# Five rearrangements in a two-layer decoder kernel: the order of weight adds in the last attention head, the pacing of the first and last scans, one PSUM bank, the place of a norm, and what the next pair's parts queue behind

## The chip, the cores and the metric

The kernel runs on one core of one Trainium2 chip. The metric is the time on the device in microseconds (us) of one execution, the median of several runs. A profile is a trace of one execution. In it PE is TensorE (matmuls), PEld its weight loads, ACT is ScalarE, DVE is VectorE, POOL is GpSimd and SP is SyncE, which only issues DMAs. The engines run their own queues in order and wait for each other through semaphores.

## The reference, cut to what matters

Two layers work on x of 512 tokens by 2048 channels, each as x + mixer(rmsnorm(x)) * silu(gate) @ w_out.

Layer 0 is differential attention with 8 heads: projections to q, k, v and a gate, a norm and a rotation of q and k, two causal softmaxes whose difference weighs v, a norm per head, the gate and an output projection.

Layer 1 is gated RWKV-7: projections to r, k, v and a gate and two low-rank ones (decay and learning rate), then for each of 32 heads of 64 channels a recurrence over the 512 tokens:

```
S = S * w_t + (S a_t) b_t^T + v_t k_t^T
y_t = S r_t
```

y is normed over the 64 channels of its head (mean and variance), a bonus term is added, and it is gated and projected.

## The kernel before, in words

All large products are made of three fp32r matmuls each (high times high, high times low, low times high), so each weight block is loaded raw by a DMA (`wraw`, or the tiles `Ta` to `Td`), copied to a high part by ScalarE (`wh`, line 105) and to a low part by VectorE (`wl`, line 106). The instructions are put on their engines by a scheduler that works from priorities (`high_priority(offset=...)`) and from orders written by hand: `issue_after(x)` puts an instruction behind x on the same engine.

**Side work is paced by ticks.** Every projection matmul calls `tick`. A `Chain` is a generator of side work that yields the number of ticks until its next step; the first chain in the list `g.chains` is counted down, and its step is put on TensorE behind the matmul of that tick. A chain that stands behind another one in the list is not counted down until that one is through.

**Layer 0.** The heads run one after another. In head h, `unit_head` makes the projections with a scheme of seven block products instead of eight: weight blocks are added to each other by accumulating DMAs of GpSimd (`add_w`), in place, in the tiles `Ta` to `Td` (`g.Ts`) and in blocks of their own (`b22`), and the sums of the activations stand in `g.sums`. The order is: products of a plain block, of the blocks S1 (each followed by an add to its weight), of S4 in all heads but the last, of S2 (each followed by an add), a `square` on the weights so added, and `third` on `b22`. Meanwhile the chain `attention` of head h - 1 does the softmax part: scores, `turn` (a transposition into bank "pb", line 363), `weigh`, and `turn_y`, which transposes the head's output into the same bank "pb", splits it into `yTh` and `yTl` (one buffer each, lines 398 and 400) and stores both from ScalarE's queue (line 385). In the last head (`last`, h = 7) the four adds to `b22` are issued after S1's adds and ahead of S2's. A chain `keys` (made by `turned`) transposes q and k of head h itself after a number of ticks, 16 in the last head (line 295).

**Layer 1** goes over 16 pairs of heads, j = 0 to 15, one round each. A round makes the projections v of j, k of j + 1, the gate of j - 2 and r of j + 1, of 48 ticks each (round 0 to 2 and 15 have fewer or others: 192 ticks in round 1, 144 in round 2, 96 in round 15). For a pair:

- `stage1` makes decays and keys from k and the low-rank parts. Part of it (`decays`, `queries`, `keys`) is put into `g.later` and is issued by steps of the running chain: one part whenever the chain has just issued a state update on VectorE (`g.state`), behind that update. `stage2` issues what is left.
- At tick 18 of v, `gram` makes the Gram matrices in the banks "pb" and "pc" (`gp`, line 1302); they go through DRAM to `t_solve`, where VectorE solves 31 triangular steps (lines 1359 and 1361) with a high priority; the result goes through DRAM (`td`) to `TT`.
- In the next round the chain of the pair runs: `t_combine` loads `TT`, waits `lead` ticks, transposes it into `T1` on VectorE (line 1386), 8 ticks later makes the matmuls `px` (line 1392, bank "pd", one buffer), 10 ticks later the second `px` (line 1402), and 8 ticks later starts `scan_pair`.
- `scan_pair` goes over 8 chunks of 64 tokens. In each: a matmul (line 1473), copies to `rhs` by ScalarE (1476), `gap` ticks, a matmul (1484), copies to `VS` by ScalarE (1486), `gap` ticks, a matmul (1491), the state update by VectorE (1495; 1498 in the first chunk), `gap_s` ticks. Then `outputs` makes `Y` in the two buffers of bank "pc", and `centre` subtracts the mean (`yc`).
- One round later `group_norm` squares (`ysq`, line 1539, in the buffer "thg", which others use too), sums and scales `yc`: one instruction of ScalarE and some 14 of VectorE. It is issued at the end of what follows tick 18 (`behind`). In the third chunk of the running scan, `finish_y` transposes `yc` back in bank "pd" (line 1552) and adds it to `p.y` (1554).

`stage_v` also uses bank "pd" for a sum over channels, read at line 1416. The leads and gaps:

```
full = LAG < j < D // P - 1
gaps = ((6, 8) if j > LAG + 1 else (5, 6)) if full else (5, 5) if j == 1 else (4, 5)
leads = {1: 54, LAG: 28, LAG + 1: 18}
```

LAG is 2, and other rounds have a lead of 10. The last pair's chain runs behind round 15, beside the last gate projections and the output projection.

Of the kernel before, what the change touches and what calls it, by code (L numbers as in the profile page):

```python
# [13 lines left out]
F32 = mybir.dt.float32  # L14
# [9 lines left out]
P = 128  # L24
# [4 lines left out]
NH = 8  # L29
# [98 lines left out]
class Chain:  # L128
# [7 lines left out]
    def step(self, g):  # L136
        with g.tc.high_priority(offset=SCAN):
            self.wait = next(self.steps, None)
        if g.state and g.later:
            with g.tc.issue_after(g.state.ins):  # L140
                g.later.pop(0)()
        g.state = None
        if self.wait is None:
            g.chains.remove(self)
# [318 lines left out]
NH4 = 8  # L463
KG = 2
# [66 lines left out]
def unit_head(g, aps, h, t1s, sq, turned):  # L531


    nc = g.nc
# [4 lines left out]
    N = NH4 // KG  # L539
# [31 lines left out]

    def all_groups(out, lhs, raw, start=False, end=False, then=None, added=None):
        for i in range(N):
            r = raw(i)
            products(out, lhs(i), r, start and i == 0, end and i == N - 1)
            if then:
                with g.tc.issue_after(added) if added else ExitStack():
                    added = add_w(g, r, then[0], then[1] + i * KG)
        return then and added

# [13 lines left out]
    X = pair()  # L594
    added = all_groups(X, lambda i: form("S1", i), chained, True, last, (c2, NH4))
    copy_out(g, acc[2:], X)
    b22 = []
    if last:
        for i in range(N):
            b22.append(load(i, NH4, c2))  # L600
            with g.tc.issue_after(added):
                added = add_w(g, b22[i], c2, i * KG)
    else:
        s4(X, b22, end=True)
        G, acc[:2] = gates(g)
        copy_out(g, acc[:2], X)
    all_groups(y, lambda i: form("S2", i), chained, then=(c1, NH4), added=last and added)
    if last:
# [189 lines left out]
def layer0(g, aps):  # L798
# [3 lines left out]
    with ExitStack() as cx:  # L802
# [91 lines left out]
        for h in range(NH):  # L894
# [13 lines left out]
            if h:  # L908
                values = unit_head(g, aps, h, t1s, sq, lambda: Chain(g, keys(2), 9 if h < NH - 1 else 16))
            else:  # L910
# [228 lines left out]
C = 64  # L1139
# [76 lines left out]
def stage1(g, j, k, up):  # L1216
# [24 lines left out]
    def decays():  # L1241
        nc.vector.tensor_tensor_scan(l[:].rearrange("p c t -> p (c t)"), g.rmask[:].rearrange("p c t -> p (c t)"),
                                     lw[:], 0.0, ALU.mult, ALU.add)
        nc.vector.tensor_scalar(m[:], l[:, :, C - 1], 0.5, None, ALU.mult)
        nc.vector.tensor_sub(l[:], l[:], m[:, :, None].to_broadcast([P, NC_, C]))
        nc.scalar.activation(p.E[:, :, 0], m[:], AF.Exp, scale=-1.0)
# [19 lines left out]

    g.later += [decays, queries, keys]
    return p


def stage2(g, j, r, p):

    nc = g.nc
    while g.later:
        g.later.pop(0)()
    col = lambda n: g.prm[n][:, j : j + 1]
# [185 lines left out]
def scan_pair(g, j, p, gap, gap_s, others):  # L1462
# [8 lines left out]
    for c in range(NC_):  # L1471
# [13 lines left out]
        for h, r_ in HEADS:  # L1485
            nc.scalar.copy(VS[r_, c, h, :], sm[r_, P : P + C])
        yield gap
# [46 lines left out]
def group_norm(g, j, p):  # L1534
    p.chain.finish(g)
    nc, w, yc = g.nc, g.work, p.yc
    NG = 2 * NT
    sq = w.tile([P, NG, C], F32, name="ysq", tag="thg", bufs=1)
    nc.scalar.activation(sq[:], yc[:], AF.Square)
# [7 lines left out]

def finish_y(g, j, p):
    nc, yc = g.nc, p.yc
    ps = g.ps.tile([P, 512], F32, name="pt", tag="pd", bufs=1)  # L1550
    for t in range(NT):
# [5 lines left out]
def layer1(g, aps):  # L1557
    nc, tc = g.nc, g.tc
    with ExitStack() as cx:
# [25 lines left out]
        for j in range(D // P):  # L1585
            p = pairs[j]
            if j:
# [115 lines left out]
def body(ctx, tc, nc, aps):  # L1703
    g = Ctx()
    g.nc, g.tc = nc, tc
    g.last, g.first, g.centred = None, [], None
    g.chains, g.later, g.state = [], [], None
    g.const = ctx.enter_context(tc.tile_pool(name="const", bufs=1))
# [58 lines left out]
```

## Time and profile before

| | before |
|---|---|
| median of 3 runs | 2116.36 us (2114.76 to 2117.71) |
| the profiled execution | 2118.3 us |
| its span, first to last instruction | 2116.6 us |
| mean granted TensorE clock | 0.995 |
| busy: PE, DVE, ACT, POOL | 98%, 76%, 55%, 17% |

The span is what the engines' instructions cover; the profiled execution's own time has 1.7 us around it. Layer 0 takes about the first 910 us, layer 1 the rest. The views that are used below: the waits (engine and line that waited, what ended the wait, total us, times, longest us), stretches (busy us of each engine and the number of instructions, then the granted clock, the busy share of the DMA engines and GB/s), the timeline (start us, us, engine, line, operation, output<-inputs, shapes, count, and in brackets the idle time before it), the chain that ended last, and the DMA queues (packets, MB, share of 16 engines).

### The profile page before, as it was taken

The numbers are of one execution on the slowest core, as the hardware profiler recorded it, in microseconds if no ns is written. First come the engines' busy times: TensorE is split into PE (matmuls) and PEld (weight loads), VectorE is DVE, ScalarE is ACT, GpSimd is POOL, SyncE is SP. The second block draws the span as 40 slices with busy tenths as digits, with TensorE's granted clock in tenths as the row PEclk, the third lists the DMA queues.
The fourth block names the chain that finished last, engine by engine and source line by source line (L and its number), as shares of the span: only waits on it lengthen the run. The fifth ranks groups of instructions, "written<-read, shape, count | busy, mean of one in ns | idle before, by whom it ended". The sixth has DMA issues, their size and how long they took to land.

```text
span 2116.6 us, 34038 instructions
## 1 busy us (share of the span) xinstructions
PE 2079.7 (98%) x11852; PEld 1690.7 (80%) x11852; DVE 1607.8 (76%) x4129; ACT 1155.7 (55%) x2278; POOL 360.9 (17%) x727
## 2 busy tenths in 40 slices
PE   9999999999998999999999999999999999999999
PEld 7888888888887888878777878777877787777887
DVE  6988888888887875576777777877777787766645
ACT  5765666566665543355465555565555556545322
POOL 1021110201112000101222221222222122221001
PEclk9999999999999999999999999999999999999999
DMA  8487877878779846623233332323332232345655
GB/s 269 155 174 188 180 172 187 165 187 178 171 187 184 299 142 184 146 90 95 82 83 91 91 89 85 94 80 98 95 95 85 85 98 79 108 129 178 189 158 121
DMA packets 159484, 294.60 MB, mean 139 GB/s; under 512 B 64352, under 2 KB 81760, under 8 KB 159312
## 3 DMA queue, kind: packets, MB, share of 16 engines
q1 hardware_dynamic: 110848, 184.91, 28.0%
q0 software_dynamic: 23808, 83.54, 21.6%
q10 hardware_dynamic: 24656, 23.97, 3.5%
q8 instruction: 93, 1.52, 0.3%
q14 instruction: 79, 0.65, 0.1%
HBM read 268.71 MB, written 23.66 MB: 138 GB/s over the span
## 4 chain that ended last, share of the span: by engine, by line
PE 79%; DVE 11%; ACT 5%; DMA 2%; issue 2%; ACTq 0%; SPq 0%; DVEq 0%
PE pp L122 39%; PE pp L567 21%; PE pt L122 5%; DVE wl L106 2%; ACT wh L105 1%; PE sc L122 1%; PE sm L1473 1%; PE o L122 1%; PE sm L1491 1%; DVE tmpl L1359 1%; PE sm L1484 1%; DVE Tm L1361 1%; PE gp L1302 1%; PE lora L122 1%; PE z L122 1%
## 5 line engine op out<-in xcount | busy, mean ns | idle before, releaser
L106 DVE TENSOR_TENSOR wl<-wraw,wh 128x1024 fp32r<-128x1024 f32 (+2 forms) x291 | 359.7, 1236 | 174.0 <-ACT wh L105 168.9
L105 ACT CAST wh<-wraw 128x1024 fp32r<-128x1024 f32 (+2 forms) x291 | 304.2, 1045 | 334.9 <-PE pp L122 203.7
L122 PE MATMUL pp<-hL,wh 128*128 128x512 f32 x1024 | 415.1, 405 | 0.0
L122 PE MATMUL pp<-hH,wl 128*128 128x512 f32 x1024 | 415.1, 405 | 0.0
L122 PE MATMUL pp<-hH,wh 128*128 128x512 f32 x1024 | 414.6, 405 | 0.0
L122 PEld LDWEIGHTS pp<-hH,wh 128*128 128x128 f32 x1024 | 193.7, 189 | 34.0
L122 PEld LDWEIGHTS pp<-hL,wh 128*128 128x128 f32 x1024 | 193.9, 189 | 33.6
L122 PEld LDWEIGHTS pp<-hH,wl 128*128 128x128 f32 x1024 | 193.9, 189 | 32.6
L567 PE MATMUL pp<-wh,hH 128*128 128x512 f32 x448 | 176.8, 395 | 0.0
L567 PE MATMUL pp<-wh,hL 128*128 128x512 f32 x448 | 175.7, 392 | 0.0
L122 PE MATMUL pp<-wh,hH 128*128 128x512 f32 x372 | 146.6, 395 | 1.3 <-ACT hH L1094 1.3
L122 PE MATMUL pp<-wh,hL 128*128 128x512 f32 x372 | 146.4, 394 | 0.2
L122 PE MATMUL pp<-wl,hH 128*128 128x512 f32 x372 | 146.0, 393 | 0.5 <-DVE wl L106 0.5
L1479 POOL COPY SA<-VS 64x64 f32<-64x64 f32 x224 | 67.7, 302 | 443.8 <-DVE VS L1495 390.2
L1359 DVE SCALAR_TENSOR_TENSOR tmpl<-LT,Tm 128x60 f32<-128x60 f32 (+24 forms) x496 | 133.9, 270 | 11.6
L567 PE MATMUL pp<-wl,hH 128*128 128x512 f32 x448 | 140.3, 392 | 0.0
L1361 DVE TENSOR_TENSOR Tm<-Tm,tmpl 128x60 f32<-128x60 f32 (+24 forms) x496 | 103.9, 209 | 10.8
L567 PEld LDWEIGHTS pp<-wl,hH 128*128 128x128 f32 x448 | 84.4, 188 | 17.3
L567 PEld LDWEIGHTS pp<-wh,hH 128*128 128x128 f32 x448 | 84.2, 188 | 17.2 <-issue 0.3
L567 PEld LDWEIGHTS pp<-wh,hL 128*128 128x128 f32 x448 | 84.2, 188 | 16.2
L1476 ACT COPY rhs<-sm 64x64 f32<-64x64 f32 x256 | 53.1, 208 | 73.1 <-PE sm L1473 68.9
L122 PEld LDWEIGHTS pp<-wh,hH 128*128 128x128 f32 x372 | 70.2, 189 | 16.2 <-ACT hH L1094 2.2
(397 smaller groups left out, 4399.5 us busy)
## 6 DMA issues: line engine op xcount, KB each, us to landing
wraw<-in_rw_w_in_dram SPq DMA_DIRECT2D x128, 512.0 KB
wraw<-in_da_w_in_dram SPq DMA_DIRECT2D x75, 512.0 KB
wraw<-in_da_w_in_dram POOLq DMA_DIRECT2D x28, 512.0 KB, 6.5
wraw<-in_da_w_out_dram SPq DMA_DIRECT2D x26, 512.0 KB
wraw<-in_rw_w_out_dram SPq DMA_DIRECT2D x26, 512.0 KB
Ta<-in_da_w_in_dram POOLq DMA_DIRECT2D x21, 512.0 KB, 5.5
Tb<-in_da_w_in_dram POOLq DMA_DIRECT2D x21, 512.0 KB, 5.4
Tc<-in_da_w_in_dram POOLq DMA_DIRECT2D x21, 512.0 KB, 5.4
```

Of the source, the lines that this page charges most:

```text
L105: a = nc.scalar.copy(hi[:, ks], raw[:, ks])
L106: d = nc.vector.tensor_sub(lo[:, ks], raw[:, ks], hi[:, ks].bitcast(F32))
L122: m = nc.tensor.matmul(out, a, b, start=s, stop=e, skip_group_check=skip)
L567: m = nc.tensor.matmul(out[t][:], x, wt[lo][:, k, :], start=first, stop=end and lo == 1 and k == KG - 1, skip_group_check=True)
L1302: m = nc.tensor.matmul(gp[h][:, i * P : (i + 1) * P], BK[r_, c0 + i, :, :], p.AR[r_, c0 + i, :, :], start=True, stop=True)
L1359: nc.vector.scalar_tensor_tensor(tt, LT[:, i : i + 1, i + 1 :].to_broadcast([P, s, n]), n2[:, i : i + 1], Tm[:, 0:s, i : i + 1].to_broadca ...
L1361: nc.vector.tensor_add(Tm[:, 0:s, i + 1 :], Tm[:, 0:s, i + 1 :], tt)
L1473: nc.tensor.matmul(sm[:, 0:P], both(p.G[:, c, 0]), both(VS[:, c]), start=True, stop=True)
L1476: nc.scalar.copy(rhs[r_, :], sm[r_, h * C : h * C + C])
L1479: nc.gpsimd.tensor_copy(p.SA[r_, c - 1, :], VS[r_, c, h, :])
L1484: nc.tensor.matmul(sm[:, P : P + C], both(g.TT[j % 2][:, c]), rhs[:], start=True, stop=True)
L1491: nc.tensor.matmul(sm[:, o : o + P], p.BKT[:, c, :], both(VS[:, c]), start=True, stop=True)
```

## The change

Five things, in the words of the code:

1. In the last head the four adds to `b22` are issued within S2's loop, each behind S2's add of the same index, so that adds to `g.Ts` and to `b22` alternate on GpSimd's queue. The wait of the chain `keys` in that head goes from 16 to 20 ticks.
2. The leads of pairs 0, 1 and 2 (rounds 1, 2 and 3) become 64, 18 and 42, and round 1's gaps (4, 5) instead of (5, 5). Round 15's gaps become (4, 4) instead of (4, 5); the last pair's chain gets gaps (5, 5) instead of (5, 6) and a lead of 24 instead of 20.
3. `finish_y` of the last pair but one uses bank "pc" (two buffers) instead of "pd".
4. From round 4 on, where the chain of pair j - 2 is through when the round starts, `group_norm` of that pair is issued at the round's head, behind `stage2`; its square has a buffer of its own.
5. The next pair's parts are five instead of three, and each is tagged: those that are mostly VectorE's go behind a state update as before (0), and `exponentials`, `scales` and `keys` behind a copy of `VS` by ScalarE (1).

```diff
-        if g.state and g.later:
-            with g.tc.issue_after(g.state.ins):
-                g.later.pop(0)()
-        g.state = None
+        for on, done in enumerate((g.state, g.copied)):
+            if done and g.later and g.later[0][0] == on:
+                with g.tc.issue_after(done.ins):
+                    g.later.pop(0)[1]()
+        g.state = g.copied = None
...
+            for x, k0 in [(r, then)] + ([(also[i], (c2, 0))] if also else []) if then else []:
                 with g.tc.issue_after(added) if added else ExitStack():
-                    added = add_w(g, r, then[0], then[1] + i * KG)
+                    added = add_w(g, x, k0[0], k0[1] + i * KG)
...
     if last:
-        for i in range(N):
-            b22.append(load(i, NH4, c2))
-            with g.tc.issue_after(added):
-                added = add_w(g, b22[i], c2, i * KG)
+        b22 += [load(i, NH4, c2) for i in range(N)]
...
-    all_groups(y, lambda i: form("S2", i), chained, then=(c1, NH4), added=last and added)
+    all_groups(y, lambda i: form("S2", i), chained, then=(c1, NH4), also=last and b22)
...
-lambda: Chain(g, keys(2), 9 if h < NH - 1 else 16))
+lambda: Chain(g, keys(2), 9 if h < NH - 1 else 20))
...
         nc.vector.tensor_sub(l[:], l[:], m[:, :, None].to_broadcast([P, NC_, C]))
+
+    def exponentials():
         nc.scalar.activation(p.E[:, :, 0], m[:], AF.Exp, scale=-1.0)
...
         nc.vector.tensor_mul(l[:], ch(k[:]), l[:])
+
+    def scales():
         for i in range(2):
...
-    g.later += [decays, queries, keys]
+    g.later += [(0, decays), (1, exponentials), (0, queries), (1, scales), (1, keys)]
...
-            nc.scalar.copy(VS[r_, c, h, :], sm[r_, P : P + C])
+            g.copied = nc.scalar.copy(VS[r_, c, h, :], sm[r_, P : P + C])
...
-    sq = w.tile([P, NG, C], F32, name="ysq", tag="thg", bufs=1)
+    sq = w.tile([P, NG, C], F32, name="ysq", tag="ysq", bufs=1)
...
-                gaps = ((6, 8) if j > LAG + 1 else (5, 6)) if full else (5, 5) if j == 1 else (4, 5)
-                leads = {1: 54, LAG: 28, LAG + 1: 18}
+                gaps = ((6, 8) if j > LAG + 1 else (5, 6)) if full else (4, 4) if j > LAG else (4, 5)
+                leads = {1: 64, LAG: 18, LAG + 1: 42}
...
             stage2(g, j, r, p)
-
-            def behind(m, j=j, p=p):
+            normed = j > LAG + 1 and pairs[j - 2].chain.wait is None
+            if normed:
+                group_norm(g, j - 2, pairs[j - 2])
...
-                if j > 1:
+                if j > 1 and not normed:
                     group_norm(g, j - 2, pairs[j - 2])
...
-        chain(g, j, p, 24, 5, 6, lead=20)
+        chain(g, j, p, 24, 5, 5, lead=24)
...
-                finish_y(g, j - 1, pairs[j - 1])
+                finish_y(g, j - 1, pairs[j - 1], ("pc", 2))
```

More of the change, by code (lines that the diff above doesn't have):

```diff
@@ L570, in products, with all_groups @@
                         first = False
-    def all_groups(out, lhs, raw, start=False, end=False, then=None, added=None):
+    def all_groups(out, lhs, raw, start=False, end=False, then=None, also=None):
+        added = None
         for i in range(N):
@@ L575, in all_groups @@
             products(out, lhs(i), r, start and i == 0, end and i == N - 1)
-            if then:
+            for x, k0 in [(r, then)] + ([(also[i], (c2, 0))] if also else []) if then else []:
                 with g.tc.issue_after(added) if added else ExitStack():
-                    added = add_w(g, r, then[0], then[1] + i * KG)
-        return then and added
+                    added = add_w(g, x, k0[0], k0[1] + i * KG)
     def s4(out, keep, start=False, end=False):
@@ L594, in unit_head @@
     X = pair()
-    added = all_groups(X, lambda i: form("S1", i), chained, True, last, (c2, NH4))
+    all_groups(X, lambda i: form("S1", i), chained, True, last, (c2, NH4))
     copy_out(g, acc[2:], X)
@@ L908, in layer0 @@
             if h:
-                values = unit_head(g, aps, h, t1s, sq, lambda: Chain(g, keys(2), 9 if h < NH - 1 else 16))
+                values = unit_head(g, aps, h, t1s, sq, lambda: Chain(g, keys(2), 9 if h < NH - 1 else 20))
             else:
@@ L1274, in stage2 @@
     while g.later:
-        g.later.pop(0)()
+        g.later.pop(0)[1]()
     col = lambda n: g.prm[n][:, j : j + 1]
@@ L1545, in group_norm, with finish_y @@
     nc.vector.tensor_mul(yc[:], yc[:], rs[:, :, None].to_broadcast([P, NG, C]))
-def finish_y(g, j, p):
+def finish_y(g, j, p, bank=("pd", 1)):
     nc, yc = g.nc, p.yc
-    ps = g.ps.tile([P, 512], F32, name="pt", tag="pd", bufs=1)
+    ps = g.ps.tile([P, 512], F32, name="pt", tag=bank[0], bufs=bank[1])
     for t in range(NT):
@@ L1592, in layer1, with behind @@
                 full = LAG < j < D // P - 1
-                gaps = ((6, 8) if j > LAG + 1 else (5, 6)) if full else (5, 5) if j == 1 else (4, 5)
-                leads = {1: 54, LAG: 28, LAG + 1: 18}
+                gaps = ((6, 8) if j > LAG + 1 else (5, 6)) if full else (4, 4) if j > LAG else (4, 5)
+                leads = {1: 64, LAG: 18, LAG + 1: 42}
                 chain(g, j - 1, pairs[j - 1], 5, *gaps, others, leads.get(j, GAP_D - GAP_T)).step(g)
             stage2(g, j, r, p)
-            def behind(m, j=j, p=p):
+            normed = j > LAG + 1 and pairs[j - 2].chain.wait is None
+            if normed:
+                group_norm(g, j - 2, pairs[j - 2])
+            def behind(m, j=j, p=p, normed=normed):
                 if j > 1:
@@ L1706, in body @@
     g.last, g.first, g.centred = None, [], None
-    g.chains, g.later, g.state = [], [], None
+    g.chains, g.later, g.state, g.copied = [], [], None, None
     g.const = ctx.enter_context(tc.tile_pool(name="const", bufs=1))
```

## The prediction, made before the change was run

> **What bounds the kernel now.** I read the page first, then who waits for whom on TensorE, then the granted clock and the chain around each long wait.
>
> ```profile
> span 2116.6 us, 34038 instructions
> PE 2079.7 (98%) x11852; PEld 1690.7 (80%) x11852; DVE 1607.8 (76%) x4129; ACT 1155.7 (55%) x2278; POOL 360.9 (17%) x727
> ```
>
> TensorE is busy for 2079.7 of 2116.6 us, and the change removes no matmul. What it can win is in the other 36.9 us, and in what a wait does to the clock afterwards. The waits of TensorE (what waited, on what: us in total, times, longest):
>
> ```profile
> PE pt L363 <- DVE rs_i L65: 7.0, 1, 7.0
> PE sm L1484 <- ACT rhs L1476: 6.5, 15, 0.9
> PE sm L1491 <- ACT VS L1486: 4.0, 14, 0.5
> PE px L1392 <- DVE y L1416: 2.0, 1, 2.0
> PE px L1392 <- DVE y L1554: 1.7, 1, 1.7
> PE px L1392 <- DVE T L1386: 1.5, 1, 1.5
> PE pt L295 <- ACT t L280: 0.7, 1, 0.7
> ```
>
> These seven rows, 23.4 us, are what the five edits aim at: L363 and L295 stand in the last attention head, the three px waits are the first use of a T in the combines of pairs 0, 2 and 15, and the two sm rows are the scans. The clock in stretches of 5 us (the column behind the engines is the granted clock):
>
> ```profile
> 1025.00:1030.00 5.00, 5.00 (x57) 3.83 (x53) 0.87 (x1) 3.28 (x7) 2.16 (x3) 0.66 0.31 89
> 1135.00:1140.00 5.00, 5.00 (x34) 3.47 (x34) 2.99 (x13) 1.83 (x4) 0.73 (x2) 0.66 0.49 125
> 1930.00:1935.00 5.00, 5.00 (x41) 3.81 (x41) 2.82 (x5) 3.21 (x7) 0.00 (x0) 0.54 0.82 297
> 1935.00:1940.00 5.00, 5.00 (x22) 4.16 (x21) 2.98 (x5) 4.02 (x9) 0.00 (x0) 0.78 0.41 95
> ```
>
> Behind each px wait the clock falls while TensorE is 100% busy: 5 x 0.34 = 1.7 us are lost behind the waits of pairs 0 and 2 each, and 5 x (0.46 + 0.22) = 3.4 us behind that of pair 15. So a wait of 1.5 to 2 us costs about twice itself.
>
> **First pairs: T used later.** The chains are paced in ticks, one per projection matmul; in a stretch where nothing else runs a tick is 71.66 / 316 = 0.227 us:
>
> ```profile
> 775.84 71.66 PE pp L122 x316
> 1023.15 0.44 DVE L1386 STREAM_TRANSPOSE T<-TT 64x256 f32<-64x256 f32 x1
> 1024.38 1.09 PE L1392 MATMUL px<-T,G 32*32 32x32 f32 x32 [1.99 <-DVE y L1416]
> 1073.85 0.90 DVE L1386 STREAM_TRANSPOSE T<-TT 64x256 f32<-64x256 f32 x2
> 1081.54 1.09 PE L1392 MATMUL px<-T,G 32*32 32x32 f32 x32
> ```
>
> Pair 0: the lead grows from 54 to 64, so px comes 10 ticks = 2.27 us later, with projection matmuls in between. It was waiting from 1022.39; it will come at 1024.66, behind T (1023.59) and behind y L1416, which frees the bank (before 1024.38). The wait of 1.99 and the 1.7 of clock go: -3.7. The margin is only 0.3 us, but a wait of 0.3 costs 0.3 and no clock.
>
> Pair 1: by the code px comes lead + 8 ticks into a chain and the scan starts at lead + 26; a chunk takes gap + gap + gap_s, the last one two gaps. So pair 0's chain ended at tick 54 + 26 + 7 x 15 + 10 = 195 of a round of 192, and now ends at 64 + 26 + 7 x 13 + 8 = 189. With the new lead of 18, px of pair 1 comes at tick 26 of its round, not at 3 + 28 + 8 = 39: 2.95 us earlier, and 3.7 earlier by the time saved. 1081.54 becomes 1074.9; T was there at 1074.75 and its solve starts earlier too (it queues on VectorE behind the first state update of the chain before). I count 0.
>
> Pair 2: its chain now starts at its own round's head, not 12 ticks into it, and the lead goes from 18 to 42: px at tick 50, not 38, +2.7 us of cover for a wait of 1.5. Gain 1.5 + 1.7 = -3.2. Pair 3 is next to be late, since nothing delays it:
>
> ```profile
> 1190.28 0.43 DVE L1386 STREAM_TRANSPOSE T<-TT 64x256 f32<-64x256 f32 x1 [0.45 <-DMA TT<-td]
> 1191.05 0.69 PE L1392 MATMUL px<-T,G 32*32 32x32 f32 x16
> ```
>
> T was ready 0.34 us ahead of px. TensorE now gets there 6.9 us earlier, so the solve must come 6.5 us earlier or px waits. The solve queues behind a scan update of pair 2, which moves by -6.9 + 2.7 = -4.2, and may go in front of it. I count 0, and take this for a rival.
>
> [...]
>
> **Norms at the round's head, own buffer, and parts behind copies of VS.** ScalarE's queue ahead of the first chunk's rhs in a steady round, and ahead of a later VS:
>
> ```profile
> 1259.21 0.75 ACT L1405 COPY TT<-px 32x256 f32<-32x256 f32 x2
> 1259.98 0.64 ACT L1539 ACTIVATE ysq<-yc 128x512 f32<-128x512 f32 x1
> 1260.52 1.03 ACT L105 CAST wh<-wraw 128x1024 fp32r<-128x1024 f32 x1
> 1261.57 0.43 ACT L1476 COPY rhs<-sm 64x64 f32<-64x64 f32 x2
> 1262.05 0.43 PE L1484 MATMUL sm<-rhs,TT 128*128 128x64 f32 x2 [0.47 <-ACT rhs L1476]
> 1288.45 0.22 ACT L1246 ACTIVATE E<-m 128x8 f32<-128x8 f32 x1 [0.71 <-DVE m L1244]
> 1288.69 0.44 ACT L1486 COPY VS<-sm 64x64 f32<-64x64 f32 x2
> ```
>
> The square stands 0.54 us (1259.98 to 1260.52) in front of rhs, for which TensorE waits 0.47. At the round's head its input, yc, is ready (the pair's outputs end the round before) and ScalarE is idle there, so rhs comes 0.54 earlier and the 0.47 goes. E blocks ScalarE for 0.71 + 0.24 us, waiting for m, with VS behind it; issued behind VS it cannot. Rounds of this kind are 5 to 14, and 15 has the longest wait (0.9) at the same place: I take 10 x 0.47 + 0.3 = 5.0 of the 6.5 for the square, and half of the 4.0 for E (one of several parts that can stand ahead of VS). Bounds: nothing gone (another instruction takes the place) and all 10.5. The parts end some 14 ticks later in their round; their user, the next Gram, is 18 ticks into the next, so this is covered. -7.0.
>
> **Last round.** Gaps of 4 instead of 5 take 7 ticks out of pair 14's scan while VectorE still solves pair 15. A scan wait can grow by no more than the tick taken: at most 7 x 0.227 = 1.6; I take +0.5, as these waits are short so far. px of pair 15:
>
> ```profile
> 1927.49 0.44 DVE L1386 STREAM_TRANSPOSE T<-TT 64x256 f32<-64x256 f32 x1
> 1927.96 0.75 DVE L1554 SCALAR_TENSOR_TENSOR y<-pt,prm_hgw,y 128x512 f32<-128x512 f32 x1
> 1928.77 1.09 PE L1392 MATMUL px<-T,G 32*32 32x32 f32 x32 [1.65 <-DVE y L1554]
> ```
>
> With finish_y in a scan bank px need not wait for y L1554, but T itself was ready only at 1927.93: 0.8 of the 1.65 goes, and the rest belongs to T. Against this px now comes 3 ticks earlier (lead + delay 48 instead of 44, scan 7 shorter), 0.7 us. So I leave wait and clock as they are: 0, between -5.0 (both gone) and +1.7 (another stretch at the low clock). The last scan's shorter gaps bring the outputs 10 ticks forward, where TensorE hardly waits: -0.2.
>
> **Last attention head.** The wait of 7.0 is not ended by the adds:
>
> ```profile
> 664.54 3.85 POOL L86 DMA_DIRECT2D wraw<-in_da_w_in_dram  x4
> 668.05 1.21 POOL L86 DMA_DIRECT2D Ta<-in_da_w_in_dram  x1
> 679.30 0.85 POOL L86 DMA_DIRECT2D Td<-in_da_w_in_dram  x1 [1.17 <-DVE so L377]
> 671.46 15.56 DMA ys<-yTl
> q0 software_dynamic: 817, 2.98, 97.0%
> q10 hardware_dynamic: 600, 0.29, 9.5%
> ```
>
> The last two lines are the queues from 671.5 to 687: the adds hold 97% of the DMA engines, and the small store of yTl (one buffer) creeps between them for 15.56 us; VectorE waits to write yTl again, and TensorE for VectorE. Alternating spreads eight adds differently, but they are the same eight of 512 KB, at 2.98 MB in 15.5 us or 2.7 us each; two are queued at 668 and the last two at 679, with four between: 22 us of work from 669 on. So the queue stays full until about 691 and the store should creep as before: 0, and at best -7.0 and 1.7 of clock. The second weight of each group lands later, but is not used before the square's four groups are through. Waiting 4 ticks more (0.9 us) for the keys covers the 0.7 of L295: -0.7.
>
> **Sum.** -3.7 - 3.2 - 7.0 + 0.5 - 0.2 - 0.7 = -14.3 us. The profiled execution took 2118.3 (span 2116.6 and 1.7 around it), 1.9 above the median of the runs; from the median 2116.4 the forecast is 2102.1.
>
> **The rivals.** A: alternating frees the store. For it: Ta's add no longer stands behind four others. Against: the full queue above. Then 7.0 and, as behind the other waits, 1.7 of clock go too: 2093.4.
>
> B: the T waits only move on to pairs 1 and 3. For it: the margins 0.15 and 0.34 above. Against: both solves can start earlier. The 6.9 us come back: 2109.0.
>
> C: another ScalarE instruction takes the square's place, or the order there does not change; the 7.0 stays: 2109.1.
>
> D, slower: the norm's VectorE work at the head goes in front of AR, for which the Gram matmuls wait.
>
> ```profile
> 1252.07 0.69 DVE L1277 TENSOR_TENSOR AR<-mixr,E 128x512 f32<-128x512 f32 x1
> 1254.84 2.06 PE L1302 MATMUL gp<-AR,BK 64*128 64x128 f32 x32
> 1260.64 0.69 DVE L1541 TENSOR_REDUCE var<-ysq 128x8 f32<-128x512 f32 x1 [2.65 <-ACT ysq L1539]
> 1264.83 0.69 DVE L1545 TENSOR_TENSOR yc<-yc,rsg 128x512 f32<-128x512 f32 x1
> ```
>
> The norm takes 1260.64 to 1265.52, 4.9 us, of which 1.2 are a wl: 3.7. AR has 2.08 us to spare. All of it in front delays the Gram by 1.6 us in each of 12 rounds; with 1.7 of clock behind each that is +39.6, or 2141.7. It decides from 3.3 us in front of AR on (1.2 late, 12 times, eats the 14.3). Against it: yc is there before the round starts, so most of the norm fits ahead of AR's own inputs.
>
> [...]
>
> **How the numbers follow.** Forecast 0.50, A 0.12, B 0.15, C 0.08, D 0.10, E 0.05. A measurement of this kernel tells 0.2% (4.2 us) from no change. B and C each lie 3 us beyond that bound, together they reach no change: I move 0.06 there. Faster 0.84, same 0.06, slower 0.10. The range goes from 2090 (A, and part of what pair 15 could give) to 2113 (B with half of C's 7.0): it leaves out D and the ends of A.
>
> **What would show it.** Right: no px wait over 0.3 us for pairs 0 to 3 and a clock of 1.00 behind them; rounds shorter by 0.6 to 0.7 us each; the store of yTl still at some 15 us and L363 near 7; a px wait of pair 15 that now ends with T. Wrong: a gap ahead of gp at the round heads, a px wait at pair 1 or 3, or L363 gone.

## The result and the profile after

The kernel after took 2111.14 us, median of 10 runs (2108.23 to 2113.86), the kernel before 2117.83 on the same chip (2112.64 to 2120.53): a ratio of 0.997 with an interval of 0.996 to 0.9981. That is 6.7 us less, where 14.3 had been forecast; the change is real, but small. The profiled execution took 2111.84 us, against 2118.3.

The page of after, and its waits of TensorE (what waited, on what: us in total, times, longest). Line numbers of after are 1 to 2 higher than in before, and 2 lower between 600 and 1250.

```profile
span 2110.1 us, 34038 instructions
PE 2076.8 (98%) x11852; PEld 1690.5 (80%) x11852; DVE 1602.6 (76%) x4129; ACT 1153.6 (55%) x2278; POOL 370.4 (18%) x727
```

```profile
PE sm L1475 <- DVE VS L1497: 9.7, 28, 0.8
PE pt L364 <- DVE rs_i L65: 5.8, 1, 5.8
PE sm L1486 <- ACT rhs L1478: 1.5, 4, 0.4
PE px L1394 <- DVE y L1418: 1.2, 1, 1.2
PE px L1394 <- DVE T L1388: 0.8, 1, 0.8
```

The waits of the scans for ScalarE (6.5 and 4.0 before) have gone down to 1.5. A row that had 1.2 us before stands on top now: 9.7 us of waits for the state update on VectorE, 28 times. Most of the missing gain is missing in the rounds in which these waits stand; whether the waits are what it went into is left to the experiments. The px waits are 2.0 us instead of 5.2, and L363 (now L364) is much as it was.

The clock behind px of pairs 0, 2 and 15 (columns as in the prediction; the granted clock is the third number from the end), and the Gram matmuls of pairs 5 and 15, before and after:

```profile
1026.74:1031.74 5.00, 5.00 (x43) 3.83 (x42) 3.08 (x5) 2.37 (x6) 1.47 (x2) 0.66 0.46 145
1139.00:1144.00 5.00, 5.00 (x76) 4.00 (x72) 0.00 (x0) 3.59 (x10) 3.27 (x6) 1.00 0.50 158
1921.30:1926.30 5.00, 5.00 (x76) 3.93 (x77) 4.94 (x8) 2.75 (x6) 0.00 (x0) 1.00 0.62 194
```

```profile
1251.67 2.06 PE L1304 MATMUL gp<-AR,BK 64*128 64x128 f32 x32
1865.80 2.06 PE L1304 MATMUL gp<-AR,BK 64*128 64x128 f32 x32
```

```profile
1870.62 2.06 PE L1302 MATMUL gp<-AR,BK 64*128 64x128 f32 x32
```

The low clock is gone behind pair 2 and here behind pair 15; behind pair 0 it is still there. From pair 5 to pair 15 the ten rounds take 614.13 us, 61.41 each; before it was 1870.62 - 1254.84 = 615.78, 61.58 each. The rounds are 0.17 shorter, where 0.6 to 0.7 had been forecast. Cut at the Gram matmuls, the 6.5 us between the two spans are +0.35 up to pair 0 (forecast -0.7), -3.3 from pair 0 to 4 (forecast -6.9), -1.9 from pair 4 to 15 (forecast -7.0 for these rounds), and -1.7 behind (forecast +0.3).

The new wait, in the round between the Gram matmuls of pairs 5 and 6: the third matmul of the fifth chunk, the two halves of its state update on VectorE, and the first matmul of the sixth chunk. After, then before:

```profile
1284.90 0.38 PE L1493 MATMUL sm<-VS,BKT 128*128 128x128 f32 x2
1286.85 0.27 DVE L1497 SCALAR_TENSOR_TENSOR VS<-sm,gam,Sg 64x64 f32<-64x64 f32 x1
1287.28 0.29 DVE L1497 SCALAR_TENSOR_TENSOR VS<-sm,gam,Sg 64x64 f32<-64x64 f32 x1
1287.71 0.46 PE L1475 MATMUL sm<-VS,G 128*128 128x128 f32 x2 [0.59 <-DVE VS L1497]
```

```profile
1289.18 0.49 PE L1491 MATMUL sm<-VS,BKT 128*128 128x128 f32 x2 [0.26 <-ACT VS L1486]
1290.47 0.27 DVE L1495 SCALAR_TENSOR_TENSOR VS<-sm,gam,Sg 64x64 f32<-64x64 f32 x1
1290.90 0.29 DVE L1495 SCALAR_TENSOR_TENSOR VS<-sm,gam,Sg 64x64 f32<-64x64 f32 x1
1291.36 0.43 PE L1473 MATMUL sm<-VS,G 128*128 128x128 f32 x2
```

Before, the update began 1.3 us behind the matmul that feeds it, and the next matmul started 0.17 us behind the update's end. After, where this matmul does wait, it starts 0.14 us behind the update's end (1287.71, against 1287.28 + 0.29). So of the 0.17 only some 0.03 us were to spare. After, TensorE gets to its matmul earlier, and VectorE, which is in the middle of the 31 triangular steps of the next pair, begins the update 1.95 us behind the matmul that feeds it. VectorE had become the next thing to be late.

### The profile page after: what moved, and what is told of

It is laid out like the page before. It is cut to its first block, busy times and chain, and to the rows that moved or that the text cites. A ratio compares the mean times of both kernels' runs of the same rounds, so it can differ in the third digit from the quotient of the medians.

```text
span 2110.1 us, 34038 instructions
## 1 busy us (share of the span) xinstructions
PE 2076.8 (98%) x11852; PEld 1690.5 (80%) x11852; DVE 1602.6 (76%) x4129; ACT 1153.6 (55%) x2278; POOL 370.4 (18%) x727
## 4 chain that ended last, share of the span: by engine, by line
PE 74%; DVE 17%; issue 3%; ACT 3%; DMA 2%; ACTq 0%; DVEq 0%; SPq 0%
PE pp L122 33%; PE pp L568 22%; PE pt L122 4%; DVE wl L106 4%; DVE tmpl L1361 3%; DVE Tm L1363 2%; DVE VS L1497 2%; PE gp L1304 1%; ACT wh L105 1%; PE sc L122 1%; PE o L122 1%; PE sm L1475 1%; PE lora L122 1%; PE z L122 1%; PE sm L1486 1%
## 5 line engine op out<-in xcount | busy, mean ns | idle before, releaser
L568 PE MATMUL pp<-wh,hH 128*128 128x512 f32 x448 | 176.8, 395 | 0.0
L568 PE MATMUL pp<-wh,hL 128*128 128x512 f32 x448 | 175.8, 392 | 0.0
L568 PE MATMUL pp<-wl,hH 128*128 128x512 f32 x448 | 140.4, 392 | 0.0
L568 PEld LDWEIGHTS pp<-wl,hH 128*128 128x128 f32 x448 | 84.4, 188 | 17.3
L568 PEld LDWEIGHTS pp<-wh,hH 128*128 128x128 f32 x448 | 84.2, 188 | 17.3 <-issue 0.3
L568 PEld LDWEIGHTS pp<-wh,hL 128*128 128x128 f32 x448 | 84.2, 188 | 16.3
L1488 ACT COPY VS<-sm 64x64 f32<-64x64 f32 x256 | 52.7, 206 | 71.9 <-PE sm L1486 67.3
```

Of the source, the lines that this page charges most:

```text
L568: m = nc.tensor.matmul(out[t][:], x, wt[lo][:, k, :], start=first, stop=end and lo == 1 and k == KG - 1, skip_group_check=True)
L1488: g.copied = nc.scalar.copy(VS[r_, c, h, :], sm[r_, P : P + C])
```

## The experiments

Sixteen kernels were run, each timed beside the kernel before; a ratio is to that, with its 95% interval. Names that begin with nt_ are changes to no_tags. A round is (Gram of pair 15 less Gram of pair 5) / 10 in the profile; for scan_late it is the median of the ten, as its last one is a microsecond longer than the others.

**1. Which part costs the rounds.** In no_norm only the norm's place is undone, in no_tags only the parts behind copies of VS:

```diff
-            normed = j > LAG + 1 and pairs[j - 2].chain.wait is None
+            normed = False
```

```diff
-    g.later += [(0, decays), (1, exponentials), (0, queries), (1, scales), (1, keys)]
+    g.later += [(0, first), (0, queries), (0, third)]    # first: decays, exponentials; third: scales, keys
```

> The kernel after, with part 4 undone: group_norm again at the end of what follows tick 18, in all rounds. Theory V (in a steady round VectorE is busy without a break from about 13 us to 48 us into the round, and the time at which it reaches the state updates of chunks 4 to 6 is what TensorE ends up waiting for): the wait of 0.47 us at L1486 for rhs comes back, and the new wait of 0.49 at L1475 for VS shrinks by about as much. Rounds stay within 0.2 us of 61.41, the time within 2 us of the 2111.1 of the kernel after. Rival S (the square's move did give its 0.47 a round, and the new wait comes from the parts): the 0.47 comes back and the 0.49 stays, rounds of 61.9, time 2116.

> The kernel after, with part 5 undone: three parts, all behind state updates. Theory V: E stands in front of a copy of VS again and costs 0.26 us at L1493, and the wait at L1475 in the same chunk shrinks by as much: rounds within 0.15 us of 61.41, time within 2 us of 2111.1. Rival S (the new wait of 0.49 comes from where the parts were put): it goes, and the rounds are some 0.25 to 0.5 us shorter, time 2106 to 2108.

Measured: no_norm ratio 0.9985 (0.9974 to 0.9997), rounds 61.44; no_tags 0.9954 (0.9938 to 0.997), median 2106.54, rounds 61.03. First the waits of no_norm, then those of no_tags, whose lines from 1250 on are 8 higher, and its Gram matmuls of pairs 5 and 15:

```profile
PE sm L1475 <- DVE VS L1497: 10.0, 29, 0.8
PE sm L1486 <- ACT rhs L1478: 1.5, 4, 0.4
```

```profile
PE sm L1501 <- ACT VS L1496: 3.7, 12, 0.5
PE sm L1494 <- ACT rhs L1486: 1.7, 5, 0.4
PE sm L1483 <- DVE VS L1505: 0.8, 4, 0.3
```

```profile
1248.43 2.06 PE L1312 MATMUL gp<-AR,BK 64*128 64x128 f32 x32
1858.69 2.06 PE L1312 MATMUL gp<-AR,BK 64*128 64x128 f32 x32
```

Theory V fell for no_tags: without part 5 the rounds are 0.38 shorter, not the same, and TensorE's waits for VectorE in the scans fall from 9.7 to 0.8 us. Parts 4 and 5 work against each other: 61.58 to 61.03 by part 4, back to 61.41 by part 5 (parts 1 to 3 do not touch these rounds). In no_norm neither theory's wait for rhs came back although the norm is where it was; what is left of part 4 there is the square's own buffer. The timed median of no_norm, 2115.67, lies outside the 2 us around 2111.1 that theory V gave and is higher than its rounds explain; its interval and that of after still overlap.

**2. What of part 4 does it.** nt_no_both is no_tags with the norm's place undone as well, so that of part 4 only the buffer is left.

> The kernel no_tags (after without part 5), and group_norm back at the end of what follows tick 18, the square's own buffer kept. Theory B (the square only has to be free of the buffer thg to go early on ScalarE, wherever the norm is issued): no wait for rhs at L1486 in the first chunk, rounds of 61.0 as in no_tags, time within 2 us of its 2106.5. Rival N (the place at the round's head is what moves it): the wait of 0.47 is back, rounds of 61.5, time 2112.

Measured: 0.9959 (0.9946 to 0.9972), rounds 61.01. The square now comes 7.2 us ahead of that round's Gram (1252.76) instead of 5.1 behind it:

```profile
1245.60 0.63 ACT L1549 ACTIVATE ysq<-yc 128x512 f32<-128x512 f32 x1 [3.60 <-DVE yc L1540]
```

Theory B holds. The order of ScalarE's instructions around the square is the same in both kernels: once the square need not wait for the buffer "thg", the scheduler puts it early wherever the norm is issued. So the buffer does what part 4 won, and the norm's place at the round's head does nothing that can be measured.

**3. Which half of part 5 costs, and why.** e_only puts only `exponentials` behind a copy of VS, k_only only `scales` and `keys`:

```diff
-    g.later += [(0, decays), (1, exponentials), (0, queries), (1, scales), (1, keys)]
+    g.later += [(0, decays), (1, exponentials), (0, queries), (0, third)]                # e_only
+    g.later += [(0, first), (0, queries), (1, scales), (1, keys)]                        # k_only
```

> The kernel after with one half of part 5: only exponentials goes behind a copy of VS; scales and keys stay behind a state update, as one part. Theory V2 (a round of the kernel after loses 0.39 us against no_tags because keys behind a copy of VS puts one more triangular step and a mix of v, some 0.45 us, ahead of the state update of the seventh chunk on VectorE; and freeing the copy of VS from E gains nothing, because TensorE then waits for the sixth chunk's update instead): the wait at L1493 goes, one of about 0.2 to 0.5 comes at L1475 in the sixth chunk, rounds of 61.0 as no_tags (61.03), time 2105 to 2109. Rival E (exponentials behind the copy is the costly half): rounds of 61.4, time 2111.

> The kernel after with the other half of part 5: decays and exponentials in one part behind a state update, scales and keys behind copies of VS. Theory V2: the costly half, rounds of 61.4 as in the kernel after, time 2111. Rival E: rounds of 61.0, time 2106.5.

Measured: e_only 0.9948 (0.9935 to 0.9961), rounds 61.01; k_only 0.9973 (0.9964 to 0.9982), rounds 61.45. Waits of e_only, then of k_only (lines 4 higher than in after):

```profile
PE sm L1479 <- DVE VS L1501: 3.3, 17, 0.4
PE sm L1497 <- ACT VS L1492: 0.2, 1, 0.2
```

```profile
PE sm L1497 <- ACT VS L1492: 4.8, 12, 0.5
PE sm L1479 <- DVE VS L1501: 3.6, 17, 0.4
```

V2 holds on both sides. In e_only the 3.7 us of waits for the copy of VS are gone, 3.3 of waits for the update stand in their place, and the round is what it was: E's stall was real, and taking it away won next to nothing: no_tags had 0.03 us to spare there (35.95 less 35.78 in the table, less the 0.14 above). The costly half is the other one. In us behind the round's Gram (pair 6):

| | third matmul, 5th chunk | its update ends | first matmul, 6th chunk | update of the 7th chunk ends | first matmul, 8th chunk | round |
|---|---|---|---|---|---|---|
| before | 34.36 | 36.36 | 36.53 | 47.22 | 47.46 | 61.59 |
| after | 33.21 | 35.78 | 35.92 | 47.03 | 47.17 | 61.39 |
| no_tags | 33.77 | 35.78 | 35.95 | 46.64 | 46.87 | 61.00 |
| e_only | 33.42 | 35.79 | 35.94 | 46.61 | 46.85 | 60.99 |

In the last three rows the fifth chunk's update ends at the same 35.78, however early its matmul comes: VectorE's queue sets it, and the sixth chunk starts with it. In the seventh chunk after is 0.4 later than the other two. What differs there is the order on VectorE ahead of that update. In after the gate's product (line 1441, 1449 in no_tags; its tile is called `mixv`, and the expectation of e_only calls it a mix of v) stands in front of the update, and a triangular step more; in no_tags it stands behind. In its place no_tags has a low part, `sLx`, of the same length ahead of the update (in after it comes behind), so that the difference is about the triangular step. The lines of after, then of no_tags:

```profile
1358.76 0.68 DVE L1441 SCALAR_TENSOR_TENSOR mixv<-thg,mixv 128x512 f32<-128x512 f32 x1
1359.88 0.29 DVE L1497 SCALAR_TENSOR_TENSOR VS<-sm,gam,Sg 64x64 f32<-64x64 f32 x1
1360.32 0.46 PE L1475 MATMUL sm<-VS,G 128*128 128x128 f32 x2 [0.21 <-DVE VS L1497]
```

```profile
1352.24 0.69 DVE L1102 TENSOR_TENSOR sLx<-k,sHx 128x512 fp32r<-128x512 f32 x1
1355.80 0.29 DVE L1505 SCALAR_TENSOR_TENSOR VS<-sm,gam,Sg 64x64 f32<-64x64 f32 x1
1356.27 0.73 DVE L1449 SCALAR_TENSOR_TENSOR mixv<-thg,mixv 128x512 f32<-128x512 f32 x1
1356.32 0.38 PE L1483 MATMUL sm<-VS,G 128*128 128x128 f32 x2
```

0.30 of the 0.39 us between the rounds of after and no_tags is there at the eighth chunk's first matmul (47.17 against 46.87). That the order does it is read from these lines; no run changes the order alone.

**4. Can the update be reached earlier.** y_later has finish_y one chunk later (3 becomes 4 in `others`), scan_late a lead of 19 and gaps (6, 7) in rounds 4 to 14, e_only_y is e_only with y_later's edit.

> The kernel after, with finish_y (four transposes on TensorE and 0.75 us on VectorE, L1556) one chunk later. It takes 0.75 us from in front of the state update that TensorE waits for. Theory V (the backlog as a whole): the wait of 0.49 at that update goes, but the update of the next chunk is reached at the same time as before and takes the wait over, less the 0.1 to 0.2 us it has to spare: rounds of 61.2 to 61.4, time 2109 to 2111. Rival L (only what stands directly in front counts): the 0.49 goes and nothing follows: rounds of 60.9, time 2105.7.

> The kernel after, in rounds 4 to 14 with a lead of 19 instead of 10 and gap_s 7 instead of 8: the matmul that waits (sixth chunk) comes 4 ticks, 0.9 us, later beside the same backlog of VectorE, those of the seventh and eighth 3 and 2 ticks later; the chain ends at tick 190 instead of 188 of 192. Theory V: the wait of 0.49 goes and rounds fall to about 60.9, less 0.1 for shorter cover in the early chunks: 0.4 a round in 11 rounds, time 2106.7. Rival R (VectorE's work shifts with the scan, since the solve slides in front of the updates wherever they are): the waits stay, rounds of 61.4, time 2111.

> The kernel e_only and finish_y one chunk later, which takes 0.75 us from VectorE's queue ahead of the update for which TensorE then waits, and, by the order of the instructions, leaves the queue ahead of the seventh chunk's update no longer. Theory V2: the sixth chunk's wait goes too, no scan wait over 0.2 us is left in a steady round, rounds of 60.7 to 60.8, time 2102.5 to 2104. Rival: the wait moves to the seventh chunk, as with y_later (61.35 against 61.41): rounds of 61.0, time 2106.

Measured: y_later 0.9972 (0.996 to 0.9985), rounds 61.35; scan_late 0.9994 (0.9981 to 1.0006), rounds 61.72; e_only_y 0.9959 (0.9946 to 0.9971), rounds 60.96. The waits for the update, in this order:

```profile
PE sm L1475 <- DVE VS L1497: 9.8, 27, 1.3
PE sm L1475 <- DVE VS L1497: 10.2, 18, 0.9
PE sm L1479 <- DVE VS L1501: 6.9, 19, 0.5
```

y_later came as V had it: the sixth chunk starts 0.4 earlier (35.53 behind the Gram), the seventh waits 0.44 instead, and the eighth starts at 47.15, as without the edit. e_only_y went the same way, by its rival: 46.80 against 46.85. It has the shortest rounds of all, with 6.9 us of these waits, so the sum of a row does not tell what the round loses. scan_late went against V: the delayed scan still waits, 0.66 to 0.9 us a round and now in the seventh chunk, and the rounds became 0.3 longer. By the code the triangular steps have the higher claim in the order on VectorE, so where the scan comes later they can fill the queue in front of its updates; this reading was not tested by itself.

**5. Pair 0, and the leads together.** nt_p0_late is no_tags with a lead of 72 for pair 0 and gaps (4, 4) in its round; nt_no_leads is no_tags with the leads 54, 28, 18 and gaps (5, 5) of before.

> The kernel no_tags with a lead of 72 instead of 64 for pair 0 and gaps of (4, 4) in its round, so that its scan ends where it did. px then comes 8 ticks, 1.8 us, later, and T and y L1418 were 0.8 to 1.4 us late in the five profiles. Theory: no px wait of pair 0 and a granted clock of 1.00 behind it; 0.8 to 2.9 us shorter, time 2104 to 2105.7. Rival: shorter gaps turn into scan waits, or px of pair 1 waits: time as no_tags, 2106.5.

> The kernel no_tags with the leads of pairs 0 to 2 (54, 28, 18) and round 1's gaps (5, 5) of before. Theory of the prediction: waits of 1.5 to 2 at px of pairs 0 and 2 and a stretch at the low clock behind each come back; the stretch from the Gram of pair 0 to that of pair 4, 218 to 221 in the profiles with the new leads, goes to 223, time 3 to 5 us longer than no_tags, 2109.5 to 2111.5. Rival: the waits only differ from run to run and the leads bring nothing, 2106.5.

Measured: nt_p0_late 0.9952 (0.994 to 0.9963); nt_no_leads 0.9974 (0.9962 to 0.9986). From pair 0's Gram to pair 4's: before 223.1 us, after 219.8, no_tags 218.57, nt_p0_late 217.67, nt_no_leads 220.01. Lines are 8 higher than in after, as in no_tags. px of pair 0 and the clock behind it in nt_p0_late; then px of pairs 0 and 2 in nt_no_leads and the clock behind each:

```profile
1025.36 1.09 PE L1402 MATMUL px<-T,G 32*32 32x32 f32 x32
```

```profile
1025.00:1030.00 5.00, 5.00 (x77) 3.88 (x76) 2.31 (x4) 2.88 (x5) 3.14 (x3) 1.00 0.59 190
```

```profile
1026.58 1.09 PE L1402 MATMUL px<-T,G 32*32 32x32 f32 x32 [1.90 <-DVE y L1426]
1135.09 0.69 PE L1402 MATMUL px<-T,G 32*32 32x32 f32 x16 [1.46 <-DVE T L1396]
```

```profile
1026.60:1031.60 5.00, 5.00 (x76) 4.16 (x77) 0.70 (x1) 4.40 (x8) 2.75 (x4) 1.00 0.40 114
1135.00:1140.00 5.00, 4.91 (x74) 3.85 (x74) 0.47 (x2) 2.79 (x5) 0.67 (x1) 1.00 0.55 133
```

Eight ticks more end pair 0's wait in all three profiles that have them (nt_p0_late, comb_a, comb_b). In the time this is not seen beside no_tags, in whose profile pair 0 waits 0.81 and the granted clock over the whole span is 0.999. Undoing the leads brings both waits back, as forecast; but behind waits of 1.90 and 1.46 the clock stays at 1.00 in this profile, and the stretch takes 220.01 instead of the 223 expected. Beside no_tags it costs 0.2% by the ratios, whose intervals overlap a little; 1.4 us of it stand in this stretch.

**6. The last attention head.** nt_no_alt is no_tags with part 1's order undone; nt_head_early starts the chain of head 6's attention after 20 ticks instead of 56 there; nt_ts_early does this and has the four adds to `b22` behind all of S2's.

> The kernel no_tags with the order of part 1 undone in the last attention head: the four adds to b22 behind S1's and ahead of S2's, keys still after 20 ticks. Theory of the prediction (the same eight adds in another order change nothing): the waits in this head (for the head's output at L364 and for weights at L568) stay at 4 to 7 us in sum, the stretch from the first head to the low-rank projections within 1.5 us of the 850 to 853 of the five profiles with alternating adds; time within 2 us of 2106.5. Rival A (alternating wins part of it): 2 to 3 us longer, time 2109.

> The kernel no_tags with the chain of attention of head 6 started after 20 ticks instead of 56 in the last head, 8.2 us earlier, so that its outputs are stored before the adds fill the DMA engines (from 669 on). Theory St (what costs is the store of yTl behind the adds): the wait at L364 (0.6 to 5.8 us) goes, and with it the stretch at the low clock; waits for weights at L568 stay as they are at 0.5 to 5; 3 to 6 us shorter, time 2102. Rival M (the adds and loads as a whole are late, and TensorE waits for them in one place or another; in the five profiles L364 and L568 sum to 3.9 to 5.9): the wait moves to L568 and grows there to 4 to 6, time 2106.

> The kernel nt_head_early (no part 5, attention of head 6 started 8.2 us earlier in the last head) with the four adds to b22 behind all of S2's. Theory St (stores of yTl that creep behind queued adds block VectorE and ScalarE, and TensorE waits for whichever comes next: 5.8 at L364 in one profile, 3.1 at L568 in nt_head_early with wl behind yTl L401): until S2's products are done only four adds lie on the DMA engines, the stores land in 3 to 7 us instead of 13 to 15, waits at L364 and L568 sum to under 1.5 us instead of 4 to 6, no low clock in this head, time 2100 to 2103. Rival M (the adds themselves are late): the sum stays at 4 to 6, or third waits for b22; time 2106 or more.

Measured: nt_no_alt 0.9958 (0.9946 to 0.997), nt_head_early 0.9947 (0.9934 to 0.9961), nt_ts_early 0.995 (0.9938 to 0.9961), none distinguishable from no_tags. What VectorE waited for in after, behind which stands the wait of 5.8 at L364; then TensorE's wait in nt_no_alt:

```profile
687.08 0.35 DVE L401 SCALAR_TENSOR_TENSOR yTl<-yt,subw,yTh 128x128 fp32r<-128x128 f32 x1 [7.07 <-DMA ys<-yTl]
```

```profile
PE pt L364 <- DVE rs_i L65: 6.2, 1, 6.2
```

TensorE's and VectorE's waits in nt_head_early:

```profile
PE pp L568 <- DVE wl L106: 3.6, 2, 3.1
696.33 0.61 DVE L401 SCALAR_TENSOR_TENSOR yTl<-yt,subw,yTh 128x128 fp32r<-128x128 f32 x2 [4.74 <-DMA ys<-yTl]
```

TensorE's and ScalarE's waits in nt_ts_early (ScalarE's from 650 to 720):

```profile
PE pp L568 <- ACT wh L105: 3.4, 1, 3.4
ACT wh L105 <- DMA wraw<-in_da_w_in_dram: 9.8, 3, 6.7
```

The place of the wait can be moved, its size only in part. The profile of after is not typical here. In it, as in before and nt_no_alt, the first store of yTl keeps VectorE from writing yTl again until 14.5 to 15.7 us behind its issue, and L364 waits 5.8 to 7.0. In the other 11 profiles with alternating adds and the attention chain where it was, VectorE writes again after 9.2 to 11.7, and L364 waits only 0.6 to 3.0. So alternating mostly does free the first store. But then the second store blocks for 10.4 to 13.9, and products (L568) wait for weights. The waits over 0.3 us in this stretch sum to 3.9 to 6.3 in these 12 profiles, to 7.0 in before and 6.2 in nt_no_alt; as there is only one profile of each kernel without the alternation, this gain is an indication and no more, and the times do not show it.

Starting the attention earlier ends L364's wait, and a later store of yTl then blocks VectorE in front of a weight's low part. With the adds in two groups that is gone too, and TensorE waits 3.4 for a weight for whose load ScalarE waits 6.7; by the code its buffer comes free only behind the later adds. So St is right on the mechanism in the first two, and M on the sum. A second buffer for yTl would test St best; it was not tried.

**7. The last round, and what adds up.** nt_no_tail is no_tags with the last round's gaps, the last chain's gaps and lead, and bank "pd" as before; comb_a is no_tags with nt_p0_late's and nt_ts_early's edits, comb_b that without the last round's.

> The kernel no_tags with the last round's gaps (4, 5), the last chain's gaps (5, 6) and lead 20, and finish_y of pair 14 in bank pd, as before. Theory of the prediction (all this comes to +0.3): px of pair 15 waits for y L1556 instead of T, 0.8 longer, tail (Gram of pair 15 to the end) within 1.5 us of the 244 it has in profiles without a stretch at the low clock, time within 1.5 us of 2106.5. Rival: the bank saves a wait long enough to drop the clock: wait 1.7 and a stretch at the low clock, time 2109 to 2111.

> The kernel no_tags with pair 0's lead of 72 and its round's gaps (4, 4), attention of head 6 started after 20 ticks in the last head, and the adds to b22 behind all of S2's. If what the profiles show adds up: 0.8 to 2.9 for px of pair 0 and 0 to 2 for the last head: 2103 to 2105. Rival: the last head waits for weights in another place and T waits come and go: 2106.5.

> comb_a with the last round's edits undone (gaps (4, 5), lead 20, gaps (5, 6), bank pd). By the prediction's terms within 1.5 us of comb_a; if bank pd costs a wait of 1.7 and a stretch at the low clock, 2.5 to 4 us longer than comb_a.

Measured: 0.9967 (0.9955 to 0.9979), 0.994 (0.9928 to 0.9953), 0.9938 (0.9926 to 0.9951). In nt_no_tail it is not px that waits but finish_y's transposes, and a stretch of 3.41 us at the low clock follows:

```profile
1921.39 0.71 PE L1562 MATMUL pt<-ident,yc 128*128 128x128 f32 x4 [2.52 <-DVE yc L1555]
```

From pair 15's Gram to the end it takes 245.3 us, 243.6 without what the low clock costs (half of 3.41, as the granted clock in a low stretch of before and after is 0.50). Counted like this, before takes 242.6 (245.99 less half of 6.83), comb_b 243.7, after 244.3, and the 15 profiles with the last round's edits 243.1 to 245.5, 244.2 on average: the edits do not shorten the work. Stretches at a low clock come there in 6 of these 15, and in all 3 that don't have them (before, nt_no_tail, comb_b). comb_a and comb_b have the lowest ratios of all: 2106.97 and 2107.27 us, where the kernel before took 2120.0 beside them, and their intervals lie below that of after (0.996 to 0.9981). They beat both kernels; that they beat no_tags is not shown.

## Why the prediction was half right

- **Direction and reach.** Faster was right, and 2111.1 lies in the range (2090 to 2113); the size was wrong by more than half, in two terms.
- **The steady rounds, -7.0: the step that failed most.** Of its two parts the square's 5.0 was right: 61.58 to 61.03 is 0.55 a round, 5.5 in ten. The mechanism was half right, since the buffer alone does it. The 2.0 for E did not come, and part 5 as a whole takes 0.38 a round back, 3.8 in ten. Two things were missed. First, "E blocks ScalarE ..., with VS behind it; issued behind VS it cannot" is true and was followed no further: the question what is late next was asked for T of pair 3 and not here, where the update on VectorE leaves some 0.03 us to spare. So this half of part 5 is worth about nothing (e_only 61.01, no_tags 61.03). Second, moving `scales` and `keys` was given no cost, and it is this half that costs: k_only has rounds of 61.45. And "half of the 4.0" was taken between bounds of 0 and 10.5, with no end for a loss, although the edit moved VectorE's instructions too.
- **Pair 0, -3.7: measured -0.84.** The margin of 0.3 us had two errors. Ten ticks were counted as ten matmuls, 2.27 us; in the order of TensorE's instructions only seven were added, as px already stood three behind its tick. And T came some 0.75 later against the rest, as the load of TT landed later: its second half went from 1023.15 to 1024.20, while VectorE's last instruction before T moved by only 0.29 (1018.98 to 1019.27). y, which frees the bank, stands behind T in VectorE's queue and came later with it.

```profile
1023.10 0.44 DVE L1388 STREAM_TRANSPOSE T<-TT 64x256 f32<-64x256 f32 x1 [2.60 <-DMA TT<-td]
1024.20 0.44 DVE L1388 STREAM_TRANSPOSE T<-TT 64x256 f32<-64x256 f32 x1
1024.67 0.69 DVE L1418 TENSOR_TENSOR y<-pt,mixv 128x512 f32<-128x512 f32 x1
1025.42 1.09 PE L1394 MATMUL px<-T,G 32*32 32x32 f32 x32 [1.15 <-DVE y L1418]
```

The low clock behind it stayed as well (0.66 in the 5 us from 1026.74), so none of the 1.7 was won here.

- **Pair 2, -3.2, and pairs 1 and 3, 0: right.** px of pair 2 starts at 1138.73 with no wait and the clock at 1.00 behind; pairs 1 and 3 do not wait, so rival B did not come. The stretch from pair 0 to 4 gained 3.3: 0.84 and 3.2, less 0.7. Of this 0.7 some 0.4 stands in the waits of the scans, which are longer there in sum (one of 0.81, for a state update at 1164.3, is new); the rest is open.
- **Pair 15, 0, and the last round, +0.3: right on average.** The wait ended with T, as said, and was 0.85 instead of 1.65. The -1.7 measured behind pair 15's Gram is luck of this one profile: the low clock stayed away in it and came back in 6 of the 15 with the same edits.
- **Last head, 0: right for the time, by luck for the store.** In the profile of after the store creeps on as said (14.5 us, L364 5.8). In the other 11 profiles with alternating adds it lands sooner, as rival A had it, but most of what L364 gains is then lost at the next store and at the weights. **Keys, -0.7: wrong.** The wait at L296 is still 0.7 us. It stands at the third block's transposes, which the attention chain makes, and the 20 ticks delay those of the first two.
- **Rivals C and D** did not come: the square left its place, and no gap stands ahead of gp at the round heads.

## What to carry to other kernels

When a stall on one engine is taken away, look in the same trace at how far the next input of the waiting engine is ahead, less what passes from that input to its use where there is a wait: here 0.17 less 0.14, so 0.03 us was all that could be won. Where parts of another engine's work are moved along with it, count the change in its queue as a possible loss, and undo edits of one change one by one, since a part that costs hides behind one that wins. Count a lead in instructions between two points of the real order, not in the ticks of the code.

## What the runs showed of the hardware

**When the clock falls.** The prediction had a wait of 1.5 to 2 us cost twice itself. In before and after the granted clock in a low stretch is 0.50, and the stretches behind px last 3.41 us, or 6.83 behind pair 15. In before they stand at 1025.83 to 1029.25 behind pair 0's wait of 1.99, 1135.06 to 1138.47 behind pair 2's of 1.5 and 1930.36 to 1937.19 behind pair 15's of 1.65; in after there is one, 1026.75 to 1030.16 behind pair 0's of 1.15. But the clock stays at 1.00 behind pair 15's wait of 0.85 in after, and behind the waits of 1.90 and 1.46 in nt_no_leads. In 18 profiles the px of pairs 0 and 2 give 36 cases; eleven have a low stretch. So the wait's length alone does not decide. What decides was not shown, and no run was made to test it. The low clock goes with the waits, as the prediction had it, but not each time.

**What a stall costs beyond itself.** In no_tags TensorE waits 0.28 us for the copy of VS before the fifth chunk's third matmul. From the last projection matmul ahead of that place to the first one behind it, start to start, it takes 0.90 us; in after, with no wait there and the same instructions, 0.38. That is 0.52 for a row of 0.28. In e_only the row is 0.02 and the distance 0.65, so 0.27 is lost with hardly a row to show it. The wait for rhs that the square caused was 0.48 in its row, and without it the matmul comes 0.55 earlier (6.67 us behind pair 6's Gram in after, 7.22 in before). In all three places the row is less than what the wait costs.
